# GpSimd multiplies queries and keys by their rsqrt factor, and the FFN's entry starts its third and fourth tiles' gate products in another order

## The chip, the cores and the metric

The kernel runs on one core of one Trainium2 chip. The core has five engines with queues of their own: PE (TensorE, matrix products and transposes), DVE (VectorE), ACT (ScalarE), POOL (GpSimd) and SP (SyncE, which issues most DMAs). Each engine takes its instructions strictly in the order in which they stand in its queue, and they wait for one another by semaphores. The metric is device time in microseconds (us) for one execution of the whole program.

## What is computed

One decoder layer on 1024 tokens of width 1024, all in float32: a Mamba-2 mixer and a stick-breaking attention side by side on one input projection, one output projection, and a SwiGLU FFN. The two places that matter here, from the reference:

```python
q = rms_norm(q.reshape(bsz, seq, N_SB_HEADS, HEAD_DIM), q_norm_w)   # 16 heads of 64
k = rms_norm(k.reshape(bsz, seq, N_SB_HEADS, HEAD_DIM), k_norm_w)
# rms_norm(x, w): x * rsqrt(mean(x * x, -1) + EPS) * w
logits = einsum("bhqd,bhkd->bhqk", qb, kp) * scale
log_rem = where(strict, log_sigmoid(-logits), 0.0)
log_between = cumsum(log_rem, axis=3, reverse=True) - log_rem
weights = where(strict, exp(log_sigmoid(logits) + log_between), 0.0)
...
h = rms_norm(x, norm2_w) * (1.0 + sc2) + sh2
ffn = (silu(h @ w_gate) * (h @ w_up)) @ w_down
```

## The kernel before

Every float32 product is made as three products of rounded operands (`mm3`, L56 and after: high by high, high by low, low by high). The high part of an operand is a cast on ACT, the low part is a subtraction on DVE (`lo_of`, L65), so each operand of a product costs ACT and DVE work before PE may start.

**Stages in time.** Conditioning and the first norm take until about 85 us, the Mamba part until about 405 us, the attention runs from there to about 930 us, the output projection to about 1089 us, the FFN's gate and up products to about 1515 us, the down projection to the end.

**Attention.** There are 8 head pairs p, and for each pair 4 units u of 256 tokens. `qkv_unit` (L746) makes the queries, keys and values of one unit: 48 projection matmuls into the tile `pp`; ACT copies them into `qkraw` (L777), squares them (`sqv`, L783); DVE sums the squares per head into the 8 columns of `qkred` (L785); POOL makes the rsqrt of them by a bit trick and three Newton steps, 14 operations on 8 columns (`rsqrt`, L118 to L129, tiles `rs_v`, `rs_y`, `rs_u`); DVE multiplies `qkraw` by `rs_y`, two instructions of 128x256 (L790); PE turns the result by four transposes (`pq`, L53); ACT copies that back (L804) and makes the high parts (L807), DVE the low parts (L808). In between run the attention's blocks of the pair ahead: PE makes logits `pl`, ACT two sigmoids of them (`pr`, L843 and `be`, L844), DVE one scan of the whole row per head (L848, over 128 to 1024 columns, with the two SBUF inputs `pr` and `idz`) and one product (L850, `be` by `pr`, both in SBUF), PE the transposes `ptw`, and PE the sums `pa`. Three `pr` tiles go round.

PE's order in the attention is set by hand: atoms of work with due times are sorted, and each PE instruction is linked behind the one before it. So a transposition `pq` whose input isn't there holds up all of PE's work behind it. The order on the other engines is the Tile scheduler's; a wait at the head of an engine's queue holds what stands behind it, whatever that is. The units 0 and 1 of a pair stand beside the long scans (640 to 1024 columns) of the pair ahead, the units 2 and 3 beside short ones.

**FFN.** The gate and up products are made Strassen-like: for each of 22 tiles f the seven products M1, M6, M2, M5, M7, M3, M4 (`product`), each four `mm3`, 12 matmuls of 128x512, from a combination of weights (`left`, made by `weight_steps` and `split_left`: A11, A12, A22 as they are and the sums S1 to S4) and a combination of activations (`right`: B11, B21, T1 to T4, B22). M1 uses A11 and B11, M2 uses A12 and B21, M6 S2 and T2, M5 S1 and T1. `finish` takes a product out of PSUM: after M1 a copy `t` on ACT, after M2 the silu `sg` on ACT, after the others sums on DVE. At the entry, M1 and M2 of tiles 0 and 1 are made early, between the last transposes of the norm; then M1 and M2 of tile 2, and from there the main loop makes the five products of tiles 0 to 2 that are left, and all seven of the others. Meanwhile ACT and DVE have to make the casts of T1, T3, B22, T4 (two of 128x1024 each), T2, and the weights.

Of the kernel before, what the change touches and what calls it, by code (L numbers as in the profile page):

```python
# [10 lines left out]
AF = mybir.ActivationFunctionType  # L11
ALU = mybir.AluOpType
# [3 lines left out]
P = 128  # L16
# [5 lines left out]
HD = 64  # L22
# [7 lines left out]
def build(tc, t, dbg=None, stop=None):  # L30
    nc = tc.nc
# [6 lines left out]
    def after(inst, earlier):  # L38
        tc.add_manual_dep(inst.ins, earlier.ins.name,
                          mybir.DependencyInfo(mybir.DependencyClass.NoSync, mybir.DependencyReason.DATA),  # L40
                          reason="issue order")
# [704 lines left out]
    def qkv_unit(p, u):  # L746

        if u == 0:
            kp_t[p] = page_q("kp", "kp"), page_q("kp", "kp")
        raw = apr.tile([P, 2, 256], F32, tag="qkraw", bufs=4, name="qkraw")  # L750
        vt = v_t[p, u] = v_tiles[(4 * p + u) % 8]
        last = p == NP - 1 and u == 3
        pps = {}

        def project(t2, k):
            if k == 0:
                pps[t2] = psp.tile([P, 512], F32, tag="pp", name="pp")
            tok = slice((2 * u + t2) * P, (2 * u + t2 + 1) * P)
            w = w_pages[p, k]
            mm3(pps[t2][:, 0:384], hh[k][:, tok], hl[k][:, tok], w[:, 0], w[:, 1], k == 0, k == KT - 1)  # L760

        if last:

            for k in range(KT):
                project(0, k)
                yield
                project(1, k)
                if k < KT - 1:
                    yield
        for t2 in range(2):  # L770
            if not last:
                for k in range(KT):
                    project(t2, k)
                    if k < KT - 1:
                        yield
            pp = pps[t2]
            nc.scalar.copy(raw[:, t2], pp[:, 0:256])  # L777
            nc.scalar.copy(vt[:, t2], pp[:, 256:384])
            if t2 == 0 and not last:
                yield  # L780
        r4 = raw.rearrange("p t (a d) -> p t a d", d=HD)
        sqv = apr.tile([P, 2, 4, HD], F32, tag="sqv", bufs=1, name="sqv")
        nc.scalar.activation(sqv.rearrange("p t a d -> p t (a d)"), raw, AF.Square)  # L783
        red = tiny.tile([P, 8], F32, tag="qkred", name="qkred")
        nc.vector.tensor_reduce(out=red, in_=sqv.rearrange("p t a d -> p (t a) d"), op=ALU.add,  # L785
                                axis=mybir.AxisListType.X)
        r = rsqrt(8, red, 1.0 / HD, "qk", nc.gpsimd).rearrange("p (t a) -> p t a", a=4)
        yield
        for t2 in range(2):
            inst = nc.vector.tensor_tensor(out=r4[:, t2], in0=r4[:, t2],  # L790
                                           in1=r[:, t2].unsqueeze(2).to_broadcast([P, 4, HD]), op=ALU.mult)
            if chain["dve"] is not None:
                after(inst, chain["dve"])
        yield
        pq = psw.tile([P, 512], F32, tag="w", name="pq")
        qs = qs_t[p, u] = qs_tiles[(4 * p + u) % 4]
        tok = slice(u * 256, u * 256 + 256)
        kh, kl = kp_t[p]
        for i in range(2):
            for t2 in range(2):  # L800
                tr(pq[:, (2 * i + t2) * P:(2 * i + t2 + 1) * P], raw[:, t2, i * P:(i + 1) * P])

        turned_ = raw.rearrange("p t c -> p (t c)")
        nc.scalar.copy(turned_, pq)  # L804
        for hi, lo, src, w in ((qs[:, 0], qs[:, 1], turned_[:, 0:256], qnw),
                               (kh[:, tok], kl[:, tok], turned_[:, 256:], knw)):
            nc.scalar.activation(hi, src, AF.Copy, scale=w)  # L807
            nc.vector.scalar_tensor_tensor(out=lo, in0=src, scalar=w, in1=f32(hi), op0=ALU.mult, op1=ALU.subtract)  # L808
# [345 lines left out]
    right = {}  # L1154
# [142 lines left out]

    def split_left(f, name, src, make):
        w = make("wl").rearrange("p (h k c) -> p h k c", h=2, k=4)
        nc.scalar.copy(w[:, 0], src)  # L1300
        lo_of(w[:, 1], src, w[:, 0])
        left[f, name] = w[:, 0], w[:, 1]

    def page_w(name):
        wcount[0] += 1
# [2 lines left out]
    def weight_steps(f):  # L1308
# [16 lines left out]
        def s34():  # L1325
# [4 lines left out]
                lambda: split_left(f, "S1", s["S1"], page_w), s34, lambda: split_left(f, "S3", s["S3"], page_w),  # L1330
                lambda: split_left(f, "S4", s["S4"], page_w), lambda: whole("A22")]

    def finish(f, m):

        z, x, y = (banks.get((f, n)) for n in "ZXY")
        add = lambda out, a, b: nc.vector.tensor_tensor(out=out, in0=a, in1=b, op=ALU.add)  # L1336
        if m == "M1":
            post[f, "t"] = small("t", 4, "t1")
            nc.scalar.copy(post[f, "t"], z)
        elif m == "M2":  # L1340
            g = post[f, "g"] = small("g", 4, "sg")
            if f < 2:
                add(g, post[f, "t"], banks[f, "W"])
            nc.scalar.activation(g, g if f < 2 else z, AF.Silu)
        elif m == "M6":
            post[f, "p"] = small("p", 2, "sp")
            add(post[f, "p"], post[f, "t"], x)
        elif m == "M5":
            post[f, "q"] = small("q", 3, "sq_")
            add(post[f, "q"], post[f, "t"], y)  # L1350
        elif m == "M7":
            add(post[f, "q"], post[f, "q"], x)
        elif m == "M3":
            add(post[f, "p"], post[f, "p"], y)
            nc.scalar.activation(post[f, "p"], post[f, "p"], AF.Silu)
        else:
            t_, g, p_, q = (post.pop((f, n)) for n in "tgpq")
            add(t_, t_, x)
            nc.vector.tensor_tensor(out=g, in0=g, in1=t_, op=ALU.mult)
            nc.vector.tensor_tensor(out=q, in0=q, in1=p_, op=ALU.mult)  # L1360
            dma(out=a_s[f, :, 0:512], in_=g)
            dma(out=a_s[f, :, 512:], in_=q)


    for m in ("M1", "M2"):
        finish(0, m)
    weights_load(2, ("A11", "A12"))
    weights_load(0, ("A21", "A22", "A11", "A12"))
    for name in ("A11", "A12"):
        split_left(2, name, raws[2, name], page_n)  # L1370
    steps0 = weight_steps(0)
    for st_ in steps0[1:3]:
        st_()
    b_sums(TB - 1)
    for m in ("M1", "M2"):
        finish(1, m)
# [4 lines left out]

    def right_split(name, srcs):
        for q in range(2):
            nc.scalar.copy(right[name][0][q], srcs[q])
            lo_of(right[name][1][q], srcs[q], right[name][0][q])

    right_split("T1", hf2[0][0:2])
    steps0[4]()
    product(2, "M2")
    finish(2, "M2")  # L1390
    right_split("T3", hf2[1][0:2])
    for st_ in steps0[5:8]:
        st_()
    right_split("B22", hf2[1][2:4])
# [8 lines left out]
    for f in range(NFF):  # L1403
        ahead = []
        if f + 1 < NFF:
            ahead = weight_steps(f + 1)
            if f + 2 < NFF:
                ahead.insert(6, lambda f=f: weights_load(f + 2))
        order = [m for m in ORDER if f > 2 or m not in ("M1", "M2")]
        for n, m in enumerate(order):  # L1410
            product(f, m)
            for a in ahead[n * len(ahead) // len(order):(n + 1) * len(ahead) // len(order)]:
# [88 lines left out]
```

## Time and profile before

| what | value |
|---|---|
| median of three runs | 1769.02 us (1762.7 to 1769.55) |
| the profiled execution, its own time | 1767.17 us |
| its span in the trace | 1765.5 us |
| mean granted TensorE clock | 0.993 of full speed |
| PE busy | 1693.4 us, 96% |
| DVE busy | 1190.4 us, 67% |
| ACT busy | 841.9 us, 48% |
| POOL busy | 276.3 us, 16% |

A row of the trace's timeline gives the start, the busy time, the engine, the line of the source, the operation, the tiles out<-in with their shape, a count where like instructions follow one another, and in brackets the idle time of that engine just before and what released it. The chain of waits is followed back from the last instruction. A table of stretches gives each engine's busy time, and PEclk, the granted clock as a share of full speed.

### The profile page before, as it was taken

How to read it: one execution, taken by the hardware profiler on the slowest of the kernel's cores; microseconds unless marked ns; L12 is line 12 of the kernel's file. 1: busy time of each engine (PE TensorE's matmuls, PEld its weight loads, DVE VectorE, ACT ScalarE, POOL GpSimd, SP SyncE). 2: the span in 40 equal slices, each digit the busy share in tenths (PEclk: the TensorE clock that was granted, in tenths of full speed). 3: DMA queues.
4: the chain of work that ended last, by engine and by line, in shares of the span. 5: the costliest groups of instructions: out<-in, count | busy, mean ns of one | idle time of the engine just before them, and what ended most of it. 6: DMA issues, size and time to landing. Idle time of an engine off the chain costs nothing.

```text
span 1765.5 us, 24607 instructions
## 1 busy us (share of the span) xinstructions
PE 1693.4 (96%) x9025; PEld 1401.9 (79%) x9025; DVE 1190.4 (67%) x1781; ACT 841.9 (48%) x1659; POOL 276.3 (16%) x638
## 2 busy tenths in 40 slices
PE   3999999998999999999899999899999999999999
PEld 2777777787888888888689887788888888888887
DVE  5497795766777777777886666976676666644541
ACT  6544563545676666667574256523333333422220
POOL 2420001023312222231553700000000000000000
PEclk9999999999999999999999999999999999999999
DMA  8366455321101101110324533432232322844721
GB/s 278 109 218 203 133 173 155 119 64 40 43 12 46 45 8 46 46 29 23 113 76 144 172 121 107 147 116 84 85 113 78 96 78 72 282 159 143 238 90 48
DMA packets 175791, 192.17 MB, mean 109 GB/s; under 512 B 11559, under 2 KB 126515, under 8 KB 175670
## 3 DMA queue, kind: packets, MB, share of 16 engines
q1 hardware_dynamic: 174582, 190.07, 34.0%
q8 instruction: 71, 1.16, 0.3%
q10 hardware_dynamic: 1088, 0.52, 0.1%
q14 instruction: 50, 0.41, 0.1%
HBM read 155.88 MB, written 34.67 MB: 108 GB/s over the span
## 4 chain that ended last, share of the span: by engine, by line
PE 69%; DVE 13%; issue 6%; DMA 5%; POOL 4%; ACT 3%; SPq 0%; DVEq 0%; ACTq 0%; POOLq 0%
PE pdn L50 13%; PE pX L50 10%; PE pp L50 9%; PE pY L50 6%; PE pZ L50 6%; PE po L50 4%; PE px L50 4%; PE pa L50 3%; PE pz L50 3%; PE ptw L53 2%; PE pl L50 2%; DVE be L850 2%; PE pyd L50 2%; DVE pr L848 2%; PE pq L53 1%
## 5 line engine op out<-in xcount | busy, mean ns | idle before, releaser
L50 PE MATMUL pp<-wp,hh 128*128 128x384 f32 x1024 | 284.2, 358 | 0.2
L50 PE MATMUL pdn<-dw,ah 128*128 128x512 f32 x704 | 216.9, 389 | 1.0 <-DVE t L1336 1.0
L50 PEld LDWEIGHTS pp<-wp,hh 128*128 128x128 f32 x1024 | 172.2, 189 | 15.0 <-issue 11.8
L848 DVE TENSOR_TENSOR_SCAN pr<-pr,idz 128x256 f32<-128x256 f32 (+7 forms) x128 | 175.8, 1394 | 6.3 <-ACT pr L843 6.2
L50 PE MATMUL pp<-wp,hl 128*128 128x384 f32 x512 | 173.1, 338 | 0.0
L50 PEld LDWEIGHTS pdn<-dw,ah 128*128 128x128 f32 x704 | 132.1, 188 | 29.0 <-DVE t L1336 1.4
L50 PE MATMUL pdn<-dw,al 128*128 128x512 f32 x352 | 136.9, 389 | 0.0
L843 ACT ACTIVATE pr<-pl 128x384 f32<-128x384 f32 (+3 forms) x192 | 97.8, 509 | 77.5 <-PE pl L50 62.3
L1436 ACT CAST ah<-araw 128x1024 fp32r<-128x1024 f32 x44 | 46.4, 1054 | 142.9 <-PE pdn L50 130.9
L790 DVE TENSOR_TENSOR qkraw<-qkraw,rs_y 128x256 f32<-128x256 f32 x64 | 33.3, 559 | 119.1 <-POOL rs_y L129 119.1
L1300 ACT CAST wl<-s 128x512 fp32r<-128x512 f32 x88 | 54.7, 621 | 123.6 <-PE pX L50 42.1
L850 DVE TENSOR_TENSOR be<-be,pr 128x256 f32<-128x256 f32 (+7 forms) x128 | 104.5, 836 | 7.1
L65 DVE TENSOR_TENSOR wl<-s,wl 128x512 fp32r<-128x512 f32 x88 | 60.6, 691 | 67.0 <-ACT wl L1300 66.3
L865 ACT COPY wt<-ptw 128x512 f32<-128x512 f32 (+1 forms) x160 | 87.5, 561 | 26.9 <-PE ptw L53 26.7
L844 ACT ACTIVATE be<-pl 128x384 f32<-128x384 f32 (+3 forms) x192 | 99.0, 516 | 0.0
L50 PEld LDWEIGHTS pp<-wp,hl 128*128 128x128 f32 x512 | 96.4, 188 | 0.2 <-issue 0.2
L65 DVE TENSOR_TENSOR al<-araw,ah 128x1024 fp32r<-128x1024 f32 x44 | 53.7, 1222 | 59.4 <-ACT ah L1436 57.5
L53 PE MATMUL ptw<-ident,be 128*128 128x128 f32 x576 | 89.3, 274 | 2.5 <-DVE be L850 2.5
L50 PE MATMUL pz<-zw,hh 128*128 128x512 f32 x256 | 90.4, 421 | 0.0
L1300 ACT CAST wl<-raw 128x512 fp32r<-128x512 f32 x62 | 38.4, 621 | 98.8 <-PE pY L50 41.6
L50 PE MATMUL px<-hh,xhi 128*128 128x512 f32 x192 | 79.4, 413 | 1.7 <-ACT hh L329 1.2
L50 PE MATMUL po<-wb,yhi 128*128 128x512 f32 x256 | 80.9, 397 | 0.0
(373 smaller groups left out, 4035.2 us busy)
## 6 DMA issues: line engine op xcount, KB each, us to landing
araw<-a_s SPq DMA_DIRECT2D x44, 512.0 KB, 3.5
adaraw<-in_w_ada_dram SPq DMA_DIRECT2D x64, 256.0 KB, 3.4
wraw<-in_w_in_dram SPq DMA_DIRECT2D x64, 192.0 KB, 2.7
raw<-in_w_gate_dram SPq DMA_DIRECT2D x46, 256.0 KB, 2.9
raw<-in_w_up_dram SPq DMA_DIRECT2D x44, 256.0 KB, 3.1
draw<-in_w_down_dram SPq DMA_DIRECT2D x44, 256.0 KB, 3.4
ada_raw<-in_w_ada_dram SPq DMA_DIRECT2D x16, 512.0 KB, 6.3
seg<-csT_s SPq DMA_DIRECT2D x32, 256.0 KB, 3.3
```

Source lines behind the costliest of these rows:

```text
L50: link(nc.tensor.matmul(out, lhsT, rhs, start=start, stop=stop, skip_group_check=more))
L53: link(nc.tensor.transpose(out=out, in_=in_, identity=identity or ident))
L65: return nc.vector.tensor_tensor(out=lo, in0=src, in1=f32(hi), op=ALU.subtract)
L790: inst = nc.vector.tensor_tensor(out=r4[:, t2], in0=r4[:, t2], in1=r[:, t2].unsqueeze(2).to_broadcast([P, 4, HD]), op=ALU.mult)
L843: nc.scalar.activation(pr[:, c0:c1], pl[:, 0:c1 - c0], AF.Sigmoid, scale=-1.0)
L844: nc.scalar.activation(be[:, c0:c1], pl[:, 0:c1 - c0], AF.Sigmoid)
L848: nc.vector.tensor_tensor_scan(out=rev, data0=rev, data1=idz[:, S - n:][:, ::-1], initial=0.0, op0=ALU.mult, op1=ALU.max)
L850: nc.vector.tensor_tensor(out=be[:, 0:n], in0=be[:, 0:n], in1=pr[:, 1:n + 1], op=ALU.mult)
L865: nc.scalar.copy(wt[:, 0:m], pt[:, 0:m])
L1300: nc.scalar.copy(w[:, 0], src)
L1436: nc.scalar.copy(ah, raw)
```

## The change

Two changes. In `qkv_unit` the product of `qkraw` and `rs_y` goes from DVE to POOL, two instructions of 128x256 in each of the 32 units. At the FFN's entry the loads of the weights A11 and A12 of tiles 2 and 3 are issued first (two loads of 256 KB more than before), the casts of both tiles are written ahead of the taking out of tile 0's products, the silu of tile 0 is ordered behind the last cast of tile 2, M1 and M2 of tile 3 are moved up from tile 3's turn in the loop to stand behind M2 of tile 2, and the casts of T1 are ordered behind the cast of S2 of tile 0.

```diff
@@ qkv_unit @@
         for t2 in range(2):
-            inst = nc.vector.tensor_tensor(out=r4[:, t2], in0=r4[:, t2],
-                                           in1=r[:, t2].unsqueeze(2).to_broadcast([P, 4, HD]), op=ALU.mult)
-            if chain["dve"] is not None:
-                after(inst, chain["dve"])
+            nc.gpsimd.tensor_tensor(out=r4[:, t2], in0=r4[:, t2],
+                                    in1=r[:, t2].unsqueeze(2).to_broadcast([P, 4, HD]), op=ALU.mult)
@@ split_left: returns the cast; finish @@
-            nc.scalar.activation(g, g if f < 2 else z, AF.Silu)
+            inst = nc.scalar.activation(g, g if f < 2 else z, AF.Silu)
+            if f == 0:
+                after(inst, entry["last"])
@@ entry @@
+    weights_load(2, ("A11", "A12"))
+    weights_load(3, ("A11", "A12"))
+    weights_load(0, ("A21", "A22", "A11", "A12"))
+    for f in (2, 3):
+        for name in ("A11", "A12"):
+            cast = split_left(f, name, raws[f, name], page_n)
+            if f == 2:
+                entry["last"] = cast
     for m in ("M1", "M2"):
         finish(0, m)
-    weights_load(2, ("A11", "A12"))
-    weights_load(0, ("A21", "A22", "A11", "A12"))
-    for name in ("A11", "A12"):
-        split_left(2, name, raws[2, name], page_n)
     steps0 = weight_steps(0)
-    for st_ in steps0[1:3]:
-        st_()
+    steps0[1]()
+    entry["last"] = steps0[2]()
...
     def right_split(name, srcs):
         for q in range(2):
-            nc.scalar.copy(right[name][0][q], srcs[q])
+            inst = nc.scalar.copy(right[name][0][q], srcs[q])
+            if name == "T1":
+                after(inst, entry["last"])
...
     product(2, "M2")
     finish(2, "M2")
+    product(3, "M1")
+    finish(3, "M1")
     right_split("T3", hf2[1][0:2])
+    product(3, "M2")
+    finish(3, "M2")
...
-        order = [m for m in ORDER if f > 2 or m not in ("M1", "M2")]
+        order = [m for m in ORDER if f > 3 or m not in ("M1", "M2")]
```

**DVE in the attention, unit 0 of a pair.** `pr` and `be` are the tiles of the scans and their products, `qv` and `kp` hold the queries and keys. Before:

```order
L850 TENSOR_TENSOR be<-be,pr_3166 128x640
L785 TENSOR_REDUCE qkred<-sqv 128x8
L790 TENSOR_TENSOR qkraw<-qkraw,rs_y 128x256 x2
L848 SCALAR_TENSOR_TENSOR pr_3167<-pr_3167,idz 128x768
L848 SCALAR_TENSOR_TENSOR pr_3165<-pr_3165,idz 128x768
L850 TENSOR_TENSOR be<-be,pr_3167 128x768
L850 TENSOR_TENSOR be<-be,pr_3165 128x768
L808 SCALAR_TENSOR_TENSOR qv<-qkraw,cols_79,qv 128x256
```

And now, where the lines 846, 848 and 806 are the 848, 850 and 808 of before:

```order
L848 TENSOR_TENSOR be<-be,pr_3166 128x640
L785 TENSOR_REDUCE qkred<-sqv 128x8
L846 SCALAR_TENSOR_TENSOR pr_3167<-pr_3167,idz 128x768
L846 SCALAR_TENSOR_TENSOR pr_3165<-pr_3165,idz 128x768
L848 TENSOR_TENSOR be<-be,pr_3167 128x768
L848 TENSOR_TENSOR be<-be,pr_3165 128x768
L806 SCALAR_TENSOR_TENSOR qv<-qkraw,cols_79,qv 128x256
```

The product is gone from between the sum and the scans; nothing else on DVE changes its place there.

**POOL in the attention, the end of one unit's rsqrt and the start of the next.** Before:

```order
L127 TENSOR_TENSOR rs_u<-rs_u,rs_v 128x8
L128 TENSOR_SCALAR rs_u<-rs_u 128x8
L129 TENSOR_TENSOR rs_y<-rs_u,rs_y 128x8
L118 TENSOR_SCALAR rs_v<-qkred 128x8
L119 TENSOR_SCALAR rs_y<-rs_v 128x8
```

And now:

```order
L128 TENSOR_SCALAR rs_u<-rs_u 128x8
L129 TENSOR_TENSOR rs_y<-rs_u,rs_y 128x8
L790 TENSOR_TENSOR qkraw<-qkraw,rs_y 128x256 x2
L118 TENSOR_SCALAR rs_v<-qkred 128x8
L119 TENSOR_SCALAR rs_y<-rs_v 128x8
```

The two products stand right behind the last step of the rsqrt.

**ACT at the FFN's entry.** `wl` are cast weights, `t` the copies after M1, `sg` the silus after M2. Before:

```order
L1384 CAST T1h<-hf_10325 128x1024
L1384 CAST T1h<-hf_10326 128x1024
L1339 COPY t_11326<-pZ 128x512
L1339 COPY t_11370<-pZ 128x512
L1212 CAST T2h<-t_11357 128x2x128
L1212 CAST T2h<-t_11361 128x2x128
L1344 ACT_TABLE_LOAD
L1344 ACTIVATE sg<-sg 128x512
L1300 CAST wl<-raw 128x512 x2
L1344 ACTIVATE sg<-sg 128x512
L1384 CAST T3h<-hf_10329 128x1024
```

And now, in two pieces; between them stand the casts of T3 and the first of B22:

```order
L1340 COPY t_11354<-pZ 128x512
L1210 CAST T2h<-t_11367 128x2x128
L1210 CAST T2h<-t_11371 128x2x128
L1340 COPY t_11380<-pZ 128x512
L1298 CAST wl<-raw 128x512 x2
L1345 ACT_TABLE_LOAD
L1345 ACTIVATE sg<-sg 128x512
L1298 CAST wl<-raw 128x512 x2
L1345 ACTIVATE sg<-sg 128x512
L1340 COPY t_11414<-pZ 128x512
L1391 CAST T3h<-hf_10329 128x1024
```

```order
L1345 ACTIVATE sg<-pZ 128x512
L1391 CAST B22h<-hf_10332 128x1024
L1340 COPY t_11450<-pZ 128x512
L1298 CAST wl<-s 128x512
L1391 CAST T4h<-hf_10327 128x1024
L1391 CAST T4h<-hf_10328 128x1024
L1345 ACTIVATE sg<-pZ 128x512
L1298 CAST wl<-s 128x512
L1391 CAST T1h<-hf_10325 128x1024
```

The casts of T1 went from first to behind T4's; the casts of tile 2's weights came ahead of the table load and the first silu, those of tile 3 (new here) ahead of the second silu. The last `wl<-s` is the cast of S2, which M6 of tile 0 reads; it now stands behind T4's casts and the silu of tile 3. On PE the four products M1, M2 of tile 2 and M1, M2 of tile 3 follow one another, and then M6 of tile 0.

## Rows read from the trace of the kernel before

**Rows 1.** The page: the chain of waits that ended last, shares by engine.
```profile
PE 69%; DVE 13%; issue 6%; DMA 5%; POOL 4%; ACT 3%; SPq 0%; DVEq 0%; ACTq 0%; POOLq 0%
```
**Rows 2.** Page, costliest groups: DVE's product; busy us, mean ns, idle before.
```profile
L790 DVE TENSOR_TENSOR qkraw<-qkraw,rs_y 128x256 f32<-128x256 f32 x64 | 33.3, 559 | 119.1 <-POOL rs_y L129 119.1
```
**Rows 3.** Waits of the whole span: who waits for whom, total us, times, longest.
```profile
PE pq L53 <- DVE qkraw L790: 13.2, 15, 4.8
```
**Rows 4.** Timeline of DVE, 496 to 526 us, units 0 and 1 of a pair.
```profile
496.60 0.68 DVE L785 TENSOR_REDUCE qkred<-sqv 128x8 f32<-128x512 f32 x1
501.26 0.76 DVE L790 TENSOR_TENSOR qkraw<-qkraw,rs_y 128x256 f32<-128x256 f32 x2 [3.98 <-POOL rs_y L129]
501.94 3.40 DVE L848 TENSOR_TENSOR_SCAN pr<-pr,idz 128x768 f32<-128x768 f32 x2
505.25 1.80 DVE L850 TENSOR_TENSOR be<-be,pr 128x768 f32<-128x768 f32 x2
...
514.12 0.68 DVE L785 TENSOR_REDUCE qkred<-sqv 128x8 f32<-128x512 f32 x1
518.77 0.76 DVE L790 TENSOR_TENSOR qkraw<-qkraw,rs_y 128x256 f32<-128x256 f32 x2 [3.98 <-POOL rs_y L129]
519.45 4.47 DVE L848 TENSOR_TENSOR_SCAN pr<-pr,idz 128x1024 f32<-128x1024 f32 x2
523.83 2.33 DVE L850 TENSOR_TENSOR be<-be,pr 128x1024 f32<-128x1024 f32 x2
```
**Rows 5.** Timeline of POOL, first and last of unit 0's 14 operations.
```profile
497.37 0.20 POOL L118 TENSOR_SCALAR rs_v<-qkred 128x8 f32<-128x8 f32 x1 [13.55 <-DVE qkred L785]
...
501.03 0.20 POOL L129 TENSOR_TENSOR rs_y<-rs_u,rs_y 128x8 f32<-128x8 f32 x1
```
**Rows 6.** Timeline of PE (unit 0's transposes) and of ACT (sigmoids ahead of scans).
```profile
501.83 0.79 PE L53 MATMUL pq<-ident,qkraw 128*128 128x128 f32 x4 [0.47 <-DVE qkraw L790]
497.86 0.53 ACT L843 ACTIVATE pr<-pl 128x384 f32<-128x384 f32 x1
517.43 0.63 ACT L843 ACTIVATE pr<-pl 128x512 f32<-128x512 f32 x1
```
**Rows 7.** Timeline of POOL and DVE where the two overlap.
```profile
390.09 0.69 DVE L632 TENSOR_TENSOR yy<-yy,sz 128x512 f32<-128x512 f32 x1
390.19 0.65 POOL L127 TENSOR_TENSOR rs_u<-rs_u,rs_v 128x8 f32<-128x8 f32 x1
889.10 3.41 DVE L848 TENSOR_TENSOR_SCAN pr<-pr,idz 128x768 f32<-128x768 f32 x2 [1.57 <-ACT pr L843]
891.13 2.18 POOL L989 TENSOR_TENSOR x<-x 128x384 f32<-128x384 f32 x1 [4.42 <-ACT x L987]
```
**Rows 8.** Timeline of POOL: a two-input product with DVE idle.
```profile
925.49 0.99 POOL L989 TENSOR_TENSOR x<-x 128x384 f32<-128x384 f32 x1 [7.81 <-ACT x L987]
```
**Rows 9.** Timeline of PE: unit 3 of the first pair.
```profile
417.20 1.35 PE L53 MATMUL pq<-ident,qkraw 128*128 128x128 f32 x4 [4.77 <-DVE qkraw L790]
```
**Rows 10.** Stretches: length, busy us of PE, PEld, DVE, ACT, POOL; PEclk.
```profile
1101.86:1129.95 28.09, 21.75 (x85) 16.65 (x86) 27.51 (x44) 18.66 (x28) 0.00 (x0) 0.94 0.38 113
416.70:420.10 3.40, 2.90 (x10) 2.50 (x10) 3.30 (x8) 1.49 (x3) 0.00 (x0) 0.52 0.00 0
1106.00:1110.00 4.00, 4.00 (x11) 2.85 (x12) 3.96 (x6) 3.63 (x6) 0.00 (x0) 0.57 0.37 100
```
**Rows 11.** Timeline of PE and ACT at the FFN's entry.
```profile
1105.82 0.50 PE L50 MATMUL pZ<-B11h,wl 128*128 128x512 f32 x1 [3.96 <-ACT wl L1300]
1111.69 0.50 PE L50 MATMUL pZ<-B21h,wl 128*128 128x512 f32 x1 [1.12 <-ACT t L1339]
1114.57 0.39 PE L50 MATMUL pX<-T2h,wl 128*128 128x512 f32 x1
1098.73 2.03 ACT L1384 CAST T1h<-hf 128x1024 fp32r<-128x1024 f32 x2
1103.34 1.28 ACT L1344 ACT_TABLE_LOAD   x1
```

More of the change, by code (lines that the diff above doesn't have):

```diff
@@ L1299, in split_left @@
         w = make("wl").rearrange("p (h k c) -> p h k c", h=2, k=4)
-        nc.scalar.copy(w[:, 0], src)
+        cast = nc.scalar.copy(w[:, 0], src)
         lo_of(w[:, 1], src, w[:, 0])
         left[f, name] = w[:, 0], w[:, 1]
+        return cast
     def page_w(name):
@@ L1331, in weight_steps @@
                 lambda: split_left(f, "S4", s["S4"], page_w), lambda: whole("A22")]
+    entry = {}
     def finish(f, m):
```

## The prediction

> **What bounds the kernel now.** I read the chain of waits first: more than two thirds of it is PE and 13% DVE [rows 1], so the time is PE's work plus the places where PE stands still, and what the change does has to be looked for in those places. Then the costliest groups: the product that leaves DVE is 33.3 us of DVE's busy time, and ahead of it DVE stands for 119.1 us, waiting for POOL's rsqrt [rows 2]. That looks like a large prize, but PE waits for this product for only 13.2 us in all, 15 times [rows 3]: of the 32 units 14 are the units 0 and 1 of seven pairs, and one is the last unit of the first pair; the units 2 and 3 have their transposes late enough to hide the chain. So the attention can win at most 13 us on that wait, and only if the product came earlier.
>
> The timeline of one pair shows why the wait of units 0 and 1 is there. Unit 0: DVE sums the squares until 497.28; POOL's 14 operations start at 497.37, one every 0.28 us (0.20 busy), and end at 501.23 [rows 4, 5]; DVE, its product at the head of its queue, does nothing for 3.98 us, multiplies until 502.02, and only then scans [rows 4]. PE's transposes start at 501.83 with no work left before them [rows 6]. Unit 1 is alike: the sum ends at 514.80, the products at 519.53, the scans of 1024 columns follow [rows 4].
>
> What matters most is a thing that DVE's idleness hides: **what POOL does while DVE works.** At 390.19 POOL starts one of the 8-column operations, which takes 0.20 us elsewhere; DVE is in a product of two SBUF tiles since 390.09, and POOL's operation takes 0.65 us and ends 0.06 us after DVE's, at 390.84 against 390.78 [rows 7]. At 891.13 POOL starts a 128x384 product that takes 0.99 us with DVE idle [rows 8]; it stands beside two scans that end at 892.51, and takes 2.18 us, to 893.31, 0.80 us after the scans' end: it did next to nothing until they were over [rows 7]. So beside a scan or another DVE operation with two SBUF inputs, a POOL operation that starts meanwhile gets through only at the end of DVE's instruction. The Trainium skill has this as a shared interface: "Advanced Engine Details and Errata", section "GPSIMD Details", says that the Pool engine shares a read and a write interface with DVE and conflicts with DVE instructions that have two SBUF inputs. The rows agree as far as the conflict goes; that the whole instruction is waited out, and not single accesses, is in the rows and not on the page.
>
> **The change, part by part.** *The product's own time.* POOL has no 128x256 product before. Bounds: not under the 0.20 us of 8 columns [rows 5], not over the 0.99 us of 128x384 [rows 8]; on a straight line between these two, 0.72 us. DVE has 0.76 us for the pair [rows 4]; POOL's two take 2 x 0.72 and two gaps of 0.08 (the pitch of 0.28 less 0.20), 1.60 us. With DVE out of the way this makes the last product 0.8 us later than now.
>
> *DVE no longer waits.* It is freed of 33.3 us of work and 119.1 us of waiting. After the sum of squares its next instruction is a scan, as the order shows. The scans of unit 0 need the sigmoid that ends at 498.39 [rows 6], and not the product: they start at about 498.46 instead of 501.94, right in the middle of POOL's 14 operations. This is where the change turns against itself.
>
> *Unit 0.* From 497.0 or 497.37 to 498.46 four or five of the 14 operations get through. Then one gets through at the end of each DVE instruction: scan (1.70 each, half of 3.40), scan, product 0.90, product 0.90 [rows 4]: four operations by 498.46 + 3.40 + 1.80 = 503.7. DVE's next in its queue needs the transposes, so it stands still now, and the remaining five or six operations take 0.28 each, 1.4 to 1.7, the two products 1.6: the last ends at 506.7 to 507.0 instead of 502.02, **4.8 us later**. PE has no slack there. Bounds: 4.6, and 5.9 if one more operation is caught.
>
> *Unit 1.* DVE stands still until the sigmoid that ends at 518.06 [rows 6]; POOL's chain begins at 514.88 (0.08 after the sum), and (518.1 - 514.88)/0.28 gives 11 or 12 operations free. The 13th waits out the first scan (half of 4.47, to 520.3), the 14th the second (522.6), the first product DVE's first `be` product (half of 2.33, to 523.8, and 0.5 of its own behind it), the second one the second, to about 526.1 instead of 519.53: **6.6 us later**. Bounds: 4.2 if the products win against the `be` products, 7.5 if one more operation is caught.
>
> *Units 2 and 3.* Their transposes don't wait now, and the scans beside them are of 128 to 512 columns, so I take 0.5 us a pair for both (0 to 2.5).
>
> *The clock.* The first pair's unit 3 waits 4.77 us [rows 9], and in the 3.4 us behind it PEclk is 0.52 [rows 10], which is the lower of the two levels, 1.2 GHz; behind the 3.96 us wait at the FFN's entry it is 0.57 over 4 us [rows 10, 11]. Half speed for 3.4 us costs about 1.6 us of matmul time. The new waits of 4.8 and 6.6 us are as long as these, so two such stretches a pair, 3.2 us (0 to 3.4).
>
> Per pair 4.8 + 6.6 + 0.5 + 3.2 = 15.1 us (8.8 to 19.3); seven pairs 106 us (62 to 135). The first pair's units and the last pair's last one stand beside other work; 1 us for unit 3 of the first pair, whose wait gets longer by the product's 0.8, and 3 us either way.
>
> *The FFN's entry.* Of the 28.09 us from the last early product to the first of the next tile, PE is busy 21.75, so 6.3 us stand empty [rows 10], 3.96 of it ahead of M1 of tile 2, for its cast weights, and 1.12 ahead of M2, for the copy `t` [rows 11]; the half clock takes another 1.7 (4.0 x 0.43), 8.0 in all. The cast weights come late since the two T1 casts (2.03) and the table load (1.28) stand before them on ACT [rows 11]; both now stand behind. I walked the new queues with these durations. M1 of tile 2 starts right away but waits about 1.1 for DVE's low part; M2 waits about 0.9 for its copy, which stands behind the table load and two silus; M2 of tile 3 waits 0.9 in the same way; M6 of tile 0 waits 1.5, since the cast of S2 now stands behind T4's casts and tile 3's silu; together 4.4 instead of 8.0 or a little more, and no single wait long enough for the lower clock. Moving tile 3's two products (2 x 2.9 us, 1111.69 to 1114.57 for one [rows 11]) is no gain of itself, they leave the loop where PE is full; they only fill the time in which the casts are made. **4 us gained** (1 to 6.5). The two added loads and the ones issued earlier are costed at nothing: they are hidden as long as the loads of tile 0's A21 and A22 still land before their sums; if not, up to 2 us, which is in the bound.
>
> Sum, against the profiled execution's own time: 1767.2 + 106 + 1 - 4 = 1870 us. The median of the runs, 1769.0, lies 1.8 above this execution, which changes nothing here.
>
> **The rivals.** *Half blocked.* DVE's scans leave gaps in which 8-column operations get through, and only the `be` products hold POOL up. The row at 891.13 speaks against it, but it is one 128x384 product and not an 8-column operation. Unit 0: the rsqrt ends at 501.2, one of the products is caught by the `be` products, about 2 us later; unit 1 about 1; with one half-clock stretch every pair at most, 3 to 5 us a pair and 21 to 35 in all: 1767.2 + 28 - 4 = about 1790, and up to 1830 with one scan waited out in each unit.
>
> *No blocking.* Only the longer product counts: 0.8 us in units 0 and 1 of seven pairs, 0.8 x 14 = 11, less the FFN's 4: 1775, slower than before by less than 0.5%. For it: the DVE operations that read PSUM let POOL through. Against it: scans and `be` products read SBUF twice.
>
> *DVE's freedom pays.* PE waits less because scans end 3.5 us earlier: 13% of the chain is DVE [rows 1]. The point from which it decides is whether the transposes of the units 0 and 1 come no later than now; then the time is 1767.2 - 4 less a part of the 13.2 us [rows 3], about 1757. Against it: the product itself cannot come earlier, since the rsqrt of the same length stands before it and its own time doubles.
>
> *Worse than forecast.* Scan and `be` products win every race at the end of an instruction, and POOL waits for DVE to run dry: unit 0 to 5.9, unit 1 to 7.5, and unit 3 2.5: 1767 + 135 = 1900.
>
> **How the numbers follow.** The blocking as worked out: 0.75, 1825 to 1905, with 1870 the likeliest. Half blocked 0.13, 1790 to 1830. No blocking 0.07, 1775. DVE's freedom 0.05, 1757. The range from 1795 to 1905 leaves out the last two, the lowest part of the half-blocked case and a little above, some 0.17. What can be told from no change here is about 0.5%, 9 us. Faster by more than that: 0.04. Within: 0.06, most of the no-blocking case. Slower: 0.90.
>
> **What would show it.** In the profile of the changed kernel: 8-column operations of POOL that take 1 to 2 us beside scans; the rsqrt of units 0 and 1 lasting 6 to 8 us instead of 3.9; PE's waits for `qkraw`, now POOL's, at 14 places with 4 us and more, some 80 us in all; PEclk at about 0.5 for 3.4 us behind each. At the FFN's entry, M1 of tile 2 right behind tile 1's last product, and M6 of tile 0 waiting for its cast. The forecast is wrong if POOL's operations stay at 0.20 us beside scans, or if the waits are there and the transposes have slack that I don't see.

## The result, and the profile after

The changed kernel takes 1859.4 us (1856.7 to 1864.0) against 1766.6 us for the kernel before, a ratio of 1.053 with an interval of 1.050 to 1.056: slower by 93 us. The profiled execution has a span of 1858.4 us against 1765.5.

Three marks in both traces cut the difference into stages: the sums of squares of the attention's units (first and last start), the last early product at the FFN's entry (`pW`), and the first down product (`pdn`). First the kernel after; the columns are count, shortest, median and longest duration in ns, first and last start in us.

```profile
L785 DVE TENSOR_REDUCE qkred<-sqv x32: 671/679/687, 370.2 to 956.8; 128x8 f32<-128x512 f32 x32
L50 PE MATMUL pW<-B21h,gw x16: 388/389/395, 1188.9 to 1197.8; 128*128 128x512 f32 x16
L50 PE MATMUL pdn<-dw,ah x704: 387/389/496, 1613.2 to 1853.9; 128*128 128x512 f32 x176
```

And the kernel before:

```profile
L785 DVE TENSOR_REDUCE qkred<-sqv x32: 669/678/686, 371.9 to 860.4; 128x8 f32<-128x512 f32 x32
L50 PE MATMUL pW<-B21h,gw x16: 388/389/392, 1092.6 to 1101.5; 128*128 128x512 f32 x16
L50 PE MATMUL pdn<-dw,ah x704: 387/389/496, 1520.7 to 1760.9; 128*128 128x512 f32 x176
```

From the first to the last sum of squares: 586.6 us against 488.5, **98.1 more**. From there to `pW`: 241.0 against 241.1. From `pW` to the first down product: 415.4 against 419.2, **3.8 less**. The rest is 1.3 us less in all. So the product on GpSimd costs some 98 us, all of it inside the attention, and the FFN's entry wins 3.8.

**Where the attention lost it.** Unit 0 of the same pair as [rows 4, 5], now on GpSimd's and DVE's timeline:

```profile
512.01 0.20 POOL L128 TENSOR_SCALAR rs_u<-rs_u 128x8 f32<-128x8 f32 x1
512.29 1.74 POOL L129 TENSOR_TENSOR rs_y<-rs_u,rs_y 128x8 f32<-128x8 f32 x1
514.11 1.57 POOL L122 TENSOR_TENSOR rs_u<-rs_y 128x8 f32<-128x8 f32 x1
515.75 0.84 POOL L127 TENSOR_TENSOR rs_u<-rs_u,rs_v 128x8 f32<-128x8 f32 x1
516.68 0.78 POOL L128 TENSOR_SCALAR rs_u<-rs_u 128x8 f32<-128x8 f32 x1
517.54 0.20 POOL L129 TENSOR_TENSOR rs_y<-rs_u,rs_y 128x8 f32<-128x8 f32 x1
...
518.95 1.18 POOL L790 TENSOR_TENSOR qkraw<-qkraw,rs_y 128x256 f32<-128x256 f32 x2
...
512.28 3.41 DVE L846 TENSOR_TENSOR_SCAN pr<-pr,idz 128x768 f32<-128x768 f32 x2 [1.48 <-ACT pr L841]
515.60 1.80 DVE L848 TENSOR_TENSOR be<-be,pr 128x768 f32<-128x768 f32 x2
```

Five operations on 8 columns take their 0.20 us; the sixth starts 0.01 us after DVE's first scan and lasts as long as the scan, the next three last as long as the second scan and the two products; when DVE has nothing more, the rest run at 0.20 again. Unit 1 has twelve free operations, and then:

```profile
537.58 2.07 POOL L128 TENSOR_SCALAR rs_u<-rs_u 128x8 f32<-128x8 f32 x1
539.72 2.10 POOL L129 TENSOR_TENSOR rs_y<-rs_u,rs_y 128x8 f32<-128x8 f32 x1
541.90 3.06 POOL L790 TENSOR_TENSOR qkraw<-qkraw,rs_y 128x256 f32<-128x256 f32 x2
537.36 4.47 DVE L846 TENSOR_TENSOR_SCAN pr<-pr,idz 128x1024 f32<-128x1024 f32 x2 [3.26 <-ACT pr L841]
541.75 2.75 DVE L848 TENSOR_TENSOR be<-be,pr 128x1024 f32<-128x1024 f32 x2
```

The two last steps of the rsqrt each wait out a scan, the two products each wait out one of DVE's. What PE makes of both, first its own timeline, then the waits of the whole span (the answer to [rows 3]):

```profile
519.61 1.47 PE L53 MATMUL pq<-ident,qkraw 128*128 128x128 f32 x4 [4.39 <-POOL qkraw L790]
543.48 0.48 PE L53 MATMUL pq<-ident,qkraw 128*128 128x128 f32 x1 [5.31 <-POOL qkraw L790]
545.02 0.90 PE L53 MATMUL pq<-ident,qkraw 128*128 128x128 f32 x3 [1.07 <-POOL qkraw L790]
```

```profile
DVE pr L846 <- ACT pr L841: 139.4, 60, 5.1
PE pq L53 <- POOL qkraw L790: 83.0, 24, 5.8
```

PE's wait for the product went from 13.2 us to 83.0. DVE's 119.1 us of waiting for GpSimd [rows 2] didn't turn into speed: DVE now waits 139.4 us for ACT's sigmoids (6.2 before). In the units 0 and 1 DVE stands for 1.5 and 3.3 us behind the sum until they are there; before they came 1.1 and 3.3 us behind it [rows 4, 6], and the longer wait for GpSimd covered that; what sets the waits in the other units wasn't traced. The clock followed the waits. The stretches are the time behind unit 0's wait and behind unit 1's, with PE's busy time first and PEclk third from the end:

```profile
519.60:523.00 3.40, 3.29 (x12) 2.57 (x14) 0.57 (x2) 1.50 (x3) 0.53 (x1) 0.52 0.00 0
...
543.20:546.70 3.50, 2.15 (x8) 1.76 (x9) 1.30 (x1) 0.62 (x2) 1.77 (x2) 0.52 0.00 0
546.70:550.10 3.40, 3.40 (x13) 3.40 (x12) 0.89 (x2) 1.96 (x6) 0.00 (x0) 0.50 0.00 0
```

PEclk is at its lower level for one such stretch behind unit 0 and for two behind unit 1. This pair has the least. In the seven pairs the clock falls at each of the fourteen waits, each time to 0.50 and for 3.4 to 10.2 us; the kernel before has no such stretch there. The sum over the fourteen stretches (441.0 to 447.8 us is the first, 929.1 to 939.3 the last), some of which begin in the wait itself:

```profile
sum 98.60, PE 67.49 PEld 56.24 DVE 32.38 ACT 28.35 POOL 34.65; mean PE 4.82 PEld 4.02 DVE 2.31 ACT 2.02 POOL 2.47
```

PE is busy in 67.5 of 98.6 us. Half of the 67.5, some 34 us or 4.8 a pair, is an estimate of what the clock cost.

**The FFN's entry**, PE's waits after, where [rows 11] had 3.96 and 1.12:

```profile
1199.59 0.73 PE L50 MATMUL pZ<-B11h,wl 128*128 128x512 f32 x2 [0.99 <-DVE wl L65]
1202.83 0.50 PE L50 MATMUL pZ<-B21h,wl 128*128 128x512 f32 x1 [0.68 <-ACT t L1340]
1209.24 0.50 PE L50 MATMUL pZ<-B21h,wl 128*128 128x512 f32 x1 [0.68 <-ACT t L1340]
1213.45 0.50 PE L50 MATMUL pX<-T2h,wl 128*128 128x512 f32 x1 [1.19 <-ACT wl L1298]
```

Four short waits, 3.5 us, at the places and for the reasons that the walk through the queues gave.

### The profile page after: what moved, and what is told of

Read it like the earlier page. It is cut to its first block, busy times and chain, and to the rows that moved or that the text cites. A ratio compares the mean times of both kernels' runs of the same rounds, so it can differ in the third digit from the quotient of the medians.

```text
span 1858.4 us, 24732 instructions
## 1 busy us (share of the span) xinstructions
PE 1722.3 (93%) x9025; PEld 1425.0 (77%) x9025; DVE 1177.2 (63%) x1717; ACT 841.4 (45%) x1659; POOL 393.1 (21%) x702
## 4 chain that ended last, share of the span: by engine, by line
PE 69%; DVE 9%; POOL 9%; issue 5%; DMA 4%; ACT 3%; SPq 0%; ACTq 0%; POOLq 0%; DVEq 0%
PE pdn L50 13%; PE pX L50 10%; PE pp L50 9%; PE pY L50 6%; PE pZ L50 6%; PE po L50 5%; PE px L50 5%; PE pa L50 3%; PE pz L50 3%; PE ptw L53 2%; POOL rs_y L129 2%; POOL qkraw L790 2%; PE pl L50 2%; POOL rs_u L128 2%; PE pyd L50 1%
## 5 line engine op out<-in xcount | busy, mean ns | idle before, releaser
L50 PE MATMUL pp<-wp,hh 128*128 128x384 f32 x1024 | 298.2, 373 | 0.1
L846 DVE TENSOR_TENSOR_SCAN pr<-pr,idz 128x256 f32<-128x256 f32 (+7 forms) x128 | 177.1, 1404 | 139.4 <-ACT pr L841 139.4
L50 PEld LDWEIGHTS pp<-wp,hh 128*128 128x128 f32 x1024 | 183.4, 201 | 14.7 <-issue 11.9
L50 PE MATMUL pp<-wp,hl 128*128 128x384 f32 x512 | 180.0, 352 | 0.0
L848 DVE TENSOR_TENSOR be<-be,pr 128x256 f32<-128x256 f32 (+7 forms) x128 | 113.0, 903 | 7.5 <-issue 0.5
L53 PE MATMUL pq<-ident,qkraw 128*128 128x128 f32 x128 | 31.1, 356 | 83.8 <-POOL qkraw L790 83.0
L50 PEld LDWEIGHTS pp<-wp,hl 128*128 128x128 f32 x512 | 102.1, 199 | 0.2 <-issue 0.2
L53 PEld LDWEIGHTS pq<-ident,qkraw 128*128 128x128 f32 x128 | 18.7, 170 | 94.0 <-POOL qkraw L790 93.4
L53 PEld LDWEIGHTS ptw<-ident,be 128*128 128x128 f32 x576 | 73.5, 143 | 9.7 <-DVE be L848 1.9
```

The source lines that it names most:

```text
L50: link(nc.tensor.matmul(out, lhsT, rhs, start=start, stop=stop, skip_group_check=more))
L53: link(nc.tensor.transpose(out=out, in_=in_, identity=identity or ident))
L846: nc.vector.tensor_tensor_scan(out=rev, data0=rev, data1=idz[:, S - n:][:, ::-1], initial=0.0, op0=ALU.mult, op1=ALU.max)
L848: nc.vector.tensor_tensor(out=be[:, 0:n], in0=be[:, 0:n], in1=pr[:, 1:n + 1], op=ALU.mult)
```

## The experiments

The theory: a GpSimd operation that starts beside a DVE instruction with two SBUF inputs ends only when that instruction does; before, DVE stood at the product and left GpSimd alone. The rivals: GpSimd's product is simply slower; sharing by single accesses; DVE's new order; the moved loads.

**The two halves of the change.** Only the product on GpSimd:

```diff
-            inst = nc.vector.tensor_tensor(out=r4[:, t2], in0=r4[:, t2], ...)
+            nc.gpsimd.tensor_tensor(out=r4[:, t2], in0=r4[:, t2], ...)
```

> The kernel before with the product on GpSimd alone; the FFN's entry as before. Theory (GpSimd is held up beside DVE instructions with two SBUF inputs): the whole loss of the attention and none of the FFN's gain, 1859.4 + 3.8 = about 1863 us, 76.3 us per head pair. Rival (part of the loss comes from the moved weight loads or from DVE's queue at the FFN): under 1850 us.

1866.4 us, a ratio of 1.056 (1.054 to 1.057). Its stage from `pW` to the first down product takes 419.2 us, as before, its attention 589.0.

Only the FFN's entry (the diff is the change without the lines above):

> The kernel before with the change of the FFN's entry alone; the product stays on DVE. From the two traces, the stretch from tile 1's last early product to the first down product is 415.4 us against 419.2: theory 1766.6 - 3.8 = 1762.8 us, a ratio of 0.998. Rival (the gain was there only because the attention had shifted the DMA and the conditioning work): no change, 1766.6 us.

1762.1 us, 0.997 (0.996 to 0.998). The stage takes 415.4 us, as in the changed kernel. The two parts have opposite signs, and their sum, 98.8 us less 5.5, is the change's 93.

**DVE made to stand still again.** The product on GpSimd, and behind it a copy on DVE that reads its result:

```diff
+        nc.vector.tensor_copy(out=red[:, 0:2].unsqueeze(2), in_=raw[:, :, 255:256])
```

> The product on GpSimd, the FFN's entry as before, and behind it in the program one 2-column copy on DVE that reads the product's result, so that DVE stands still during GpSimd's chain as it did before. The copy adds about 0.2 us of DVE in each unit. Theory (the loss is GpSimd held up beside DVE's scans and products): rsqrt back to 3.9 us, only the slower product is left, 0.8 to 1.0 us in units 0 and 1 of seven pairs: 1766.6 + 11 to 16 = 1778 to 1783 us. Rival (GpSimd is slow beside any engine's traffic, or the product itself is the loss): still over 1840 us.

1782.9 us, 1.008 (1.006 to 1.010). DVE waits, GpSimd's rsqrt takes 3.9 us again and its two products 1.18:

```profile
503.21 1.18 POOL L790 TENSOR_TENSOR qkraw<-qkraw,rs_y 128x256 f32<-128x256 f32 x2
504.43 0.17 DVE L792 COPY qkred<-qkraw 128x2 f32<-128x2 f32 x1 [5.27 <-POOL qkraw L790]
```

Giving DVE *more* waiting (160.9 us in all instead of 119.1) takes 83 of the 99 us away again. That the product runs on GpSimd costs 15 us, the added copy included; that DVE works meanwhile costs the rest.

**The disputed cost by itself.** Behind the last output, chains of 16 dependent GpSimd products on 8 columns beside three long DVE instructions of one kind, for five kinds (k = 0 to 4):

```diff
+                if k == 0:
+                    nc.vector.tensor_tensor_scan(out=C, data0=A, data1=B, initial=0.0, op0=ALU.mult, op1=ALU.max)
+                elif k == 1:
+                    nc.vector.tensor_tensor(out=C, in0=A, in1=B, op=ALU.mult)
+                elif k == 2:
+                    nc.vector.tensor_scalar(out=C, in0=A, scalar1=0.5, scalar2=1.0, op0=ALU.mult, op1=ALU.add)
+                elif k == 3:
+                    nc.vector.tensor_copy(out=C, in_=A)
+                else:
+                    nc.vector.tensor_tensor(out=C[:, 0:512], in0=A[:, 0:512], in1=Q, op=ALU.mult)   # Q in PSUM
+            for i in range(16):
+                nc.gpsimd.tensor_tensor(out=O[k], in0=O[k], in1=O[k], op=ALU.mult)
```

> The kernel before, with a tail behind the last output that measures the disputed cost by itself: five times, 16 dependent 8-column products on GpSimd beside three long instructions on DVE: (0) scans of 1024 columns with two SBUF inputs, (1) products of 1024 columns with two SBUF inputs, (2) a tensor-scalar operation of 1024 columns with one SBUF input, (3) copies of 1024 columns, (4) products of 512 columns of one SBUF and one PSUM input; last, three products of 128x256 on GpSimd with DVE idle. The time is that of before and some 40 us more. Theory (an instruction with two SBUF inputs holds GpSimd up until it ends): in (0) and (1) one GpSimd operation per DVE instruction, lasting 2.2 and 1.2 us, and the rest 0.20; in (2) to (4) all 0.20 us. Rival (they share single accesses): in (0) and (1) all 16 somewhat longer than 0.20 us, none as long as DVE's instruction. Second rival (any long DVE instruction on SBUF holds GpSimd up): (2) and (3) like (1). The 128x256 product alone: 0.7 us each.

GpSimd's five chains and its three products of 128x256, then the DVE instructions beside the chains (those of the fourth are like those of the third):

```profile
1768.24 10.35 POOL L1510 TENSOR_TENSOR po<-po 128x8 f32<-128x8 f32 x16 [752.80 <-DVE pC L1497]
1779.31 7.35 POOL L1510 TENSOR_TENSOR po<-po 128x8 f32<-128x8 f32 x16 [0.72 <-DVE pC L1497]
1787.37 5.76 POOL L1510 TENSOR_TENSOR po<-po 128x8 f32<-128x8 f32 x16 [0.71 <-DVE pC L1497]
1793.84 5.76 POOL L1510 TENSOR_TENSOR po<-po 128x8 f32<-128x8 f32 x16 [0.71 <-DVE pC L1497]
1800.31 4.35 POOL L1510 TENSOR_TENSOR po<-po 128x8 f32<-128x8 f32 x16 [0.71 <-DVE pC L1497]
1804.94 1.99 POOL L1515 TENSOR_TENSOR pW<-pW,pg 128x256 f32<-128x256 f32 x3 [0.28 <-DVE pg L1511]
```

```profile
1768.06 6.94 DVE L1500 TENSOR_TENSOR_SCAN pC<-pA,pB 128x1024 f32<-128x1024 f32 x3
1779.26 3.74 DVE L1502 TENSOR_TENSOR pC<-pA,pB 128x1024 f32<-128x1024 f32 x3
1787.33 2.15 DVE L1504 TENSOR_SCALAR pC<-pA 128x1024 f32<-128x1024 f32 x3
...
1800.27 2.13 DVE L1508 TENSOR_TENSOR pC<-pA,pQ 128x512 f32<-128x512 f32 x3
```

Beside the product that reads PSUM the chain takes 4.35 us, 15 times 0.277 and once 0.20: it isn't touched. Beside three scans it takes 6.0 us more, beside three products 3.0. In the single records three GpSimd operations last 2.10, 2.25 and 2.24 us beside the three scans, 1.18 beside the second and the third product, and all that start later 0.198: here one operation gets through per DVE instruction. That is the theory, and the sharing by single accesses falls. The theory was too narrow at one point, and there the second rival was right: the tensor-scalar operation and the copy, with one input, hold GpSimd up as well (1.4 us over the three, the two whole waits 0.65 each beside instructions of 0.69). They move 1024 columns in 0.69 us, where the products need 1.22. The Trainium skill, "Advanced Engine Details and Errata", section "GPSIMD Details", names both kinds, two SBUF inputs and the 2-port mode of DVE; these rows agree with it, if the mode is what makes the copy that fast, which no run here shows directly. The 128x256 product alone takes 0.61 us.

**The rsqrt on DVE, with the product on either engine.** The argument `nc.gpsimd` of `rsqrt` is dropped, so DVE makes it in 11 operations:

```diff
-        r = rsqrt(8, red, 1.0 / HD, "qk", nc.gpsimd).rearrange("p (t a) -> p t a", a=4)
+        r = rsqrt(8, red, 1.0 / HD, "qk").rearrange("p (t a) -> p t a", a=4)
```

> The kernel before with the rsqrt moved to DVE, 11 operations on 8 columns there instead of 14 on GpSimd; the product stays on DVE and the FFN's entry as before. DVE's like operations on one column take 0.16 us, one every 0.2 us where they depend on one another, so about 2.3 us for the chain instead of 3.9 and two changes of engine. Theory (what the attention can win lies in the latency of this chain in units 0 and 1, and DVE stands still for it anyway): the transposes come some 1.7 us earlier there, PE's waits for the product (13.2 us in all) go to nearly nothing: 1767.5 - 10 to 15 = 1753 to 1758 us. Rival (DVE's 25 us more of busy work delay the scans and PE waits for them instead): 1765 to 1775 us.

1747.7 us, 0.990 (0.988 to 0.992): 18.5 us faster than the kernel before, more than expected. On DVE the last step is done 2.9 us after the sum's start, where GpSimd needed 4.6 [rows 4, 5]:

```profile
489.77 0.68 DVE L785 TENSOR_REDUCE qkred<-sqv 128x8 f32<-128x512 f32 x1
...
492.50 0.17 DVE L125 SCALAR_TENSOR_TENSOR rs_y<-rs_u,rs_y 128x8 f32<-128x8 f32 x1
492.70 0.76 DVE L790 TENSOR_TENSOR qkraw<-qkraw,rs_y 128x256 f32<-128x256 f32 x2
...
494.71 0.60 PE L53 MATMUL pq<-ident,qkraw 128*128 128x128 f32 x4
```

The transposes of the units 0 and 1 no longer wait. The attention's stage is 472.2 us against 488.5; another 3.4 us go behind the last sum. There the hold works the other way round: before, the two products on DVE started 0.1 and 0.2 us after GpSimd's products of 128x1024, ended 0.3 us after them, and took 5.03 us instead of 0.76.

```profile
864.95 4.83 POOL L971 TENSOR_TENSOR y_page<-y_page 128x1024 fp32r<-128x1024 f32 x2
865.03 5.03 DVE L790 TENSOR_TENSOR qkraw<-qkraw,rs_y 128x256 f32<-128x256 f32 x2 [4.00 <-POOL rs_y L129]
```

With the rsqrt on DVE its first operation waits out one such product (2.14 us instead of 0.17) and the pair another (2.85 us), so the collision stays, but the pair ends 7.7 us after the sum's start instead of 9.7.

The same with the product on GpSimd:

> The rsqrt on DVE, only the product on GpSimd, the FFN's entry as before. Theory (a GpSimd operation waits out the DVE instruction beside it): the two units part. In unit 0 the scans' inputs are there when the rsqrt ends, so each of the two products waits out one scan of 1.7 us and runs 0.57 us behind it: the last one about 2 us later than in the kernel before. In unit 1 the scan's input comes only 3.3 us after the sum, the products are free and end about 1 us earlier than before. Per pair +1 to +3 us with the lower clock behind unit 0's wait, in all 1767.5 + 7 to 21 = 1775 to 1788 us. Rival (GpSimd's product costs only its length): both units earlier than before, 1755 to 1760 us.

1766.9 us, 1.001 (1.000 to 1.002). The two units part as the theory says. Unit 0 (GpSimd, DVE, PE), and then unit 1:

```profile
496.40 3.92 POOL L790 TENSOR_TENSOR qkraw<-qkraw,rs_y 128x256 f32<-128x256 f32 x2 [17.98 <-DVE rs_y L125]
496.15 3.77 DVE L846 TENSOR_TENSOR_SCAN pr<-pr,idz 128x768 f32<-128x768 f32 x2
500.38 0.55 PE L53 MATMUL pq<-ident,qkraw 128*128 128x128 f32 x3 [1.69 <-POOL qkraw L790]
...
515.47 1.18 POOL L790 TENSOR_TENSOR qkraw<-qkraw,rs_y 128x256 f32<-128x256 f32 x2 [15.15 <-DVE rs_y L125]
```

Beside scans the pair takes 3.92 us; started while DVE stands still, 1.18. But the time was 8 us under the expected range. At the transposes unit 0 loses 1.2 us a pair and unit 1 wins 0.8. I had put a stretch of lower clock behind unit 0's wait in every pair. Behind waits of the same 1.7 us it is there in four of the seven pairs and not in the other three; the first of the four:

```profile
565.00:568.40 3.40, 3.40 (x17) 1.83 (x17) 1.40 (x3) 1.05 (x3) 0.00 (x0) 0.50 0.00 0
```

These four pairs take 65.1 to 65.3 us, the two before them 63.6 and 63.5, against 63.3 in the kernel before. The attention is 5.9 us longer in all. Behind it 4.7 are won: the product now stands ahead of some of GpSimd's long operations, and from the last sum to `pW` it takes 236.4 us against 241.1, which the expectation hadn't in it.

**Both gains together:** rsqrt and product on DVE, and the changed FFN entry.

> The rsqrt and the product on DVE, and the changed FFN entry. If both parts are independent: the time of the DVE chain alone less the 5 us that the FFN's entry alone was measured to gain, 1748 to 1753 us, faster than both kernels of the case. Rival (the chain on DVE gains nothing): 1762 us, as with the FFN's entry alone.

1744.5 us, 0.988 (0.986 to 0.989): faster than both kernels, by 22 and by 115 us. The stage at the FFN takes 415.4 us here too. Against the DVE chain alone it gains 3.2 us and not 5, close to the 3.8 that the stage shows. In the profiled run its attention was 2.5 us longer, all of it in the first pair: there PEclk is 0.50 from 411.9 to 418.7 us, at the last unit's wait of 3.14 us, and it doesn't fall at the 3.30 us of the DVE chain alone. That run has the lower level elsewhere, for 3.4 us at its first down products. Why the clock falls at the one wait and not at the other stays open.

**Which part of the FFN's change wins.** The new order of the casts for tile 2 only, with no casts and no products of tile 3 moved up, and the product on DVE:

```diff
-    weights_load(3, ("A11", "A12"))
-    for f in (2, 3):
+    for f in (2,):
...
-    product(3, "M1")
-    finish(3, "M1")
...
-    product(3, "M2")
-    finish(3, "M2")
```

> Of the FFN's change only the new order of the casts, for tile 2 alone: loads and casts of tile 2 ahead of the first silu, T1's casts behind S2's; no casts and no products of tile 3 moved up, and the product on DVE. Theory (the new order of casts opens a hole in front of M6 of tile 0, whose S2 is now cast late, and only the products of tile 3 fill it): M1 of tile 2 starts at once, but M6 waits some 4 to 5 us and the clock falls behind that: no gain left, 1766 to 1769 us. Rival (the casts alone make the gain): 1762 us.

1765.7 us, 0.9995 (0.998 to 1.001): no gain. The stage takes 420.5 us, 1.3 more than before. M1 of tile 2 waits 0.98 us, and M6 of tile 0:

```profile
1110.23 0.80 PE L50 MATMUL pX<-T2h,wl 128*128 128x512 f32 x1 [5.05 <-ACT wl L1300]
```

The casts' order alone moves the hole of 3.96 us from in front of M1 to in front of M6, where it is 5.05, with PEclk at 0.50 for 6.8 us from 1109.3. The two products of tile 3 fill it; the gain is theirs and the order's together.

**Where the loss sits, and its dose.** The product on GpSimd in units 2 and 3 only:

```diff
+            (nc.vector if u < 2 else nc.gpsimd).tensor_tensor(out=r4[:, t2], in0=r4[:, t2], ...)
```

> The product on GpSimd in units 2 and 3 of every pair only, on DVE in units 0 and 1, the FFN's entry as before. Theory (the loss comes where the chain stands beside long scans and has no slack, units 0 and 1): GpSimd is held up a little in unit 3 too (its rsqrt took 4.6 us instead of 3.9 there in the changed kernel), but the transposes come 2 to 2.7 us behind the product, so PE doesn't notice: 1766.2 us, within 3. Rival (the loss is spread over all units, or comes from GpSimd's other work, the weight casts, being pushed back): +20 us or more.

1768.7 us, 1.000 (0.999 to 1.002), and the longest of its 32 products on GpSimd takes 1.57 us. The edit also drops the order that tied DVE's product to the work ahead of it; in the units 0 and 1 of the seven pairs the product still ends 5.4 us after the sum's start. Half of the moved products cost nothing, those with slack behind them.

The product on GpSimd in all units, the FFN's entry as before, and scans of 640 columns and more cut into two, one continuing the other:

```diff
+                        nc.vector.tensor_tensor_scan(out=rev[:, 0:half], ..., initial=0.0, ...)
+                        nc.vector.tensor_tensor_scan(out=rev[:, half:], ..., initial=rev[:, half - 1:half], ...)
```

> The product on GpSimd in all units, the FFN's entry as before, and DVE's scans of 640 columns and more cut into two halves, one continuing the other, so that a GpSimd operation waits out half as much. Compared with the product alone on GpSimd (1866.4 us). Theory (one GpSimd operation gets through at each end of a DVE instruction): unit 0 gets two operations more through while the scans run and ends 0.6 us earlier, unit 1 ends some 2.2 us earlier, 2.8 us a pair, less the fixed cost of 8 more scans a pair on DVE: about 1846 us, 1840 to 1856. Rival (what counts is how long DVE is busy, not how it is cut): 1866 us or more.

1857.5 us, 9 us less than with whole scans, and 1.5 us above the expected range: half the size that I gave it. The wait of one operation halved as expected; GpSimd in unit 0:

```profile
510.48 1.50 POOL L118 TENSOR_SCALAR rs_v<-qkred 128x8 f32<-128x8 f32 x1 [12.17 <-DVE qkred L785]
512.07 0.77 POOL L119 TENSOR_SCALAR rs_y<-rs_v 128x8 int32<-128x8 int32 x1
```

The first line shows a limit of the theory: this operation started beside a `be` product of 0.81 us and waited out the half scan behind it too, which started 0.08 us before that product ended. So not every end of a DVE instruction lets one through. The scheduler had put that `be` product behind the sum of squares, so the chain's first operation was caught already and more of the others. The mechanism that I expected isn't what came: from the last projection matmul to the last transpose unit 0 takes 5.6 us against 5.9 with whole scans and unit 1 7.5 against 7.8, some 0.5 us a pair instead of 2.8. With two things changed at once, the run supports that one operation waits half as long beside half a scan, and doesn't measure what that is worth; where the rest of the 9 us comes from isn't shown.

## Why the prediction was right, point by point

- **The reading of the idle time.** That DVE's 119 us of waiting were worth nothing, and that they protected GpSimd, held: the kernel that gives DVE its waiting back loses 15 us instead of 99.
- **The product's own time** was over-estimated: 0.61 us each, and 1.18 for the pair, since two that follow one another overlap a little, where the prediction had 1.60.
- **Unit 0**: the trace has five operations free and four caught, within the forecast. The last product ends 10.0 us after the sum's start against 5.4, **4.6 later**; the prediction had 4.8. From the last projection matmul ahead of the transposes to the last transpose it is 5.9 us against 1.3, 4.6 later too.
- **Unit 1**: the trace has twelve free, two that wait out scans and two products that wait out `be` products, as forecast. The last product ends 11.55 us after the sum's start against 5.4, **6.1 later**; to the last transpose it is 7.8 us against 1.3, 6.5 later. The 6.6 of the prediction isn't the sum of its own terms: two scans to 522.6, two `be` products to 524.9 and 0.5 behind them make 525.4 and not 526.1, 5.9 later.
- **Units 2 and 3**: no wait at their transposes, nothing instead of 0.5.
- **The clock**: the mechanism held; that the size of the term fits is partly luck. Two stretches of 3.4 us a pair were taken, 48 us in all; there are two in each pair, but of 3.4 to 10.2 us, 98.6 in all. From the first to the last of the seven pairs' unit 0 (433.2 to 897.9 us after, 433.4 to 813.1 before) a pair takes 77.45 us against 63.28, 14.2 more; less 4.6 and 6.5 at the transposes that leaves 3.1, as against 3.2. It fits because PE stands still in a third of that time, and because some 1.3 us of the clock's price lie in the transposes themselves (1.47 and 1.38 us for four instead of 0.79) and are in the 4.6 and 6.5 already.
- **Seven pairs**: 15.1 each was taken, 106 in all; it is 14.2 for six of them and less in the last, and 98.1 with the first pair's units in the stage.
- **The FFN's entry**: 4 us predicted, 3.8 measured. The four new waits were put at 1.1, 0.9, 0.9 and 1.5, and are 0.99, 0.68, 0.68 and 1.19.
- **The sum**: 103 us over the profiled execution were predicted, 93 came. Of the 10 us between them 9 are the attention's term, and the rest lies ahead of the attention and behind the FFN, where nothing was changed.
- **The rivals**: half-blocked falls with the row of 1.74 us for an 8-column operation beside a scan; no blocking and DVE's freedom fall with the 83.0 us.

## What to carry to other kernels

An engine's idle time can be what keeps another engine fast: before filling it, look in the trace for what the neighbours do while it is busy, for instance one small operation that lasts exactly as long as the large one beside it. A chain of many tiny dependent GpSimd operations suffers most beside DVE, since each of them can wait out a whole DVE instruction (1.74 us instead of 0.20); here the same chain was better on DVE, although DVE has more to do. DVE is held up by GpSimd's long operations in the same way (2.55 us for a product of 0.42 us at the attention's end), so look at both. And read a stretch of lower clock in every repetition, not in one: behind like waits of 1.7 us it came in four pairs of seven. When a change has two independent parts, cut the trace into stages before judging it: the FFN's part was good by 3.8 us and hidden under a loss of 98.

## What the runs showed that I had not expected

GpSimd waits not only for DVE instructions with two SBUF inputs: a copy and a tensor-scalar operation between SBUF tiles of 128x1024 in float32, at 0.69 us, held it up for 0.65 us each, while a product of an SBUF and a PSUM operand of 0.69 us did not hold it up at all. And the rsqrt on DVE was worth 18.5 us where 10 to 15 were expected. It also shortened the wait of the first pair's last unit, from 4.77 us [rows 9] to 3.30, with no stretch of lower clock behind it in that run where [rows 10] had one, and it shortened DVE's collisions with GpSimd's long products at the attention's end.
